# Hybrid decoder step: in the first sub-block, two spatial mixes and six folds of wo with the values are emitted later

## The chip, the core and the metric

The kernel runs on one core of one Trainium2 chip. Its time is the device time of one execution, in microseconds (us), as the median of several runs. The core has five engines that work side by side, each through its own instructions in a fixed order: PE multiplies matrices (PEld loads its stationary operand), DVE is the vector engine, ACT the scalar engine for activations and copies, POOL a second elementwise engine, and SP issues the DMAs.

## What is computed

One layer of a decoder in fp32, for 2048 new prompt tokens (D = 1024) and 32 sample tokens: a mixer with gated linear attention (GLA) and a spatial gating unit (SGU), a cross-attention to 256 memory tokens, and a gated MLP with a short convolution. The parts that the change touches:

```python
q, k, v, r, a, u, sv = split_cols(xn @ w_in)
...
o, S = gla_chunked(q, k, v, logg, s0)
o = rmsnorm(o, g_gla_out).astype(xn.dtype)
o = o.reshape(B, T, GLA_WIDTH) * jax.nn.silu(r)
u = jax.nn.gelu(u)
sv = rmsnorm(jax.nn.gelu(sv).reshape(B, T, SGU_HEADS, SGU_DH), g_sgu)
z = sgu_spatial(sv, w_s, b_s)
s_out = u * z.reshape(B, T, SGU_WIDTH)
y = jnp.concatenate([o, s_out], axis=-1) @ w_out
...
o = jnp.einsum('bhtm,bmhd->bthd', p, mv).reshape(B, T, D_MODEL)
return o @ wo_x
```

`sgu_spatial` multiplies, per head and per chunk of 128 tokens, a lower triangular 128x128 matrix with the normed values. The memory attention's last two lines are linear in the values, so the kernel multiplies the values by `wo_x` once, ahead of time, and uses the result as the weight for all tokens.

## The kernel before

The prompt is cut into four sub-blocks of 512 tokens (`s` = 0 to 3). Each sub-block goes through the projections, GLA and SGU, the output projection `wo`, the memory attention and the MLP. Products are made of three passes (`mm3`, lines 100 to 102): every fp32 operand is split into a high part and a residue (`split`, lines 85 and 86: ACT makes the high part, DVE or POOL the residue), and hi·hi, hi·lo and lo·hi are added up.

The program is written as a list of steps. `weave` takes a main list and side lists; a side list with (first, last) is spread evenly behind the main steps of these indices, and where several side lists are due behind the same main step, they follow in the order in which they are named. `run` goes through the woven list. It loads the weights of later steps up to five units ahead, and splits most of them as it loads them (`wunit`), so each weight brings a DMA on SP, an ACT instruction and a DVE instruction ahead of its step. The order in which the steps are emitted is not yet the order on an engine: the tile context is opened with `schedule_with_timeline_sim=True`, and when it is left, a pass orders each engine's instructions, with the emitted order as their priority. Each engine then runs its own in that order and waits on semaphores.

In the first sub-block the main list has 19 steps: the projections sv (0 to 3), a (4), k (5), q (6), v (7 to 10), u (11 and 12), r (13 to 16), and the first two half steps of `wo` (17 and 18), which take the SGU half of the concatenated input. Woven into it are:

- `qk_steps`: the folds of the queries' weight with the memory keys.
- `vo_steps`: eight folds of `wo_x` with the memory values, one for each head and each half of the columns (`fold_vo`). A fold reloads the head's values at its first half, and for two tiles of 128 rows makes six products of 512 columns (`vop`), evacuates them on ACT (`voh`) and DVE (`vol`), and leaves the writes to `vod` in DRAM, which SP issues later (`put` and `flush`). `vod` is read by the attention's output projection.
- `sgu_steps`: statistics and scaling of the values, then four spatial mixes, one per head (`mix`, from line 946 on). A mix makes four narrow products (`zp`, line 950), scales and shifts them on DVE (`z`, line 953), multiplies by u on POOL (line 958), and splits the result, the high part on ACT (`ch`) and the residue on POOL (`cl`). The SGU half of `wo` reads `ch` and `cl`.
- `gla_steps`: for each of two head pairs `p`, the diagonal, seven levels (0 to 6), a decay, the states and the chunk outputs. A level subtracts on DVE (`e`, line 1046), takes exponentials on ACT, makes `kr` (line 1058) and `e` times k (line 1062) on DVE, four products on PE for two heads together (`s`, line 1068; the profile counts eight instructions), and copies them under a mask to `P` on DVE (line 1072). The decay ends in POOL's `kh` (line 1104) and its transposes on PE (`ktp`, line 1107).
- `gtail`: norm (`onorm`), gating (`gate`) and transposes (`back`, `otp`, line 1217) of the GLA output, which the second half of `wo` needs.

Levels 2 to 6 and the decay of the second head pair are emitted behind main steps 12 and 13, its states and chunk outputs behind 16.

Of the kernel before, what the change touches and what calls it, by code (L numbers as in the profile page):

```python
# [38 lines left out]
def hymba_step_kernel(  # L39
# [22 lines left out]
    def U(name, dt=F32):  # L62
        return up.tile([128, TM], dt, tag="U", name=name)
# [63 lines left out]
    def wready(src, name):  # L127

        def load():
            out = []  # L130
            for x, tag in enumerate(("whi", "wlo")):
                t = wp.tile(list(src.shape[0:1]) + list(src.shape[2:]), F32R, tag=tag, name=f"{tag}_{name}")
                nc.sync.dma_start(t.bitcast(F32), src[:, x])
                out.append(t)
            return tuple(out)
        return load
# [220 lines left out]
    def keep(t, pattern, base, cm):  # L357
        pool.affine_select(out=t, in_=t, pattern=pattern, compare_op=ALU.is_ge, fill=0.0,
                           base=base, channel_multiplier=cm)
# [125 lines left out]
    def weave(main, *sides):  # L485

        out = []
        due = [0.0] * len(sides)
        at = [0] * len(sides)
        for i, m in enumerate(main):  # L490
            out.append(m)
            for j, (steps, first, last) in enumerate(sides):
                if i < first:
                    continue
                due[j] = len(steps) * min(1.0, (i - first + 1) / (last - first + 1))
                while at[j] < len(steps) and at[j] < due[j] - 1e-9:
                    out.append(steps[at[j]])
                    at[j] += 1
        for j, (steps, _, _) in enumerate(sides):
            out += steps[at[j]:]  # L500
        return out
# [158 lines left out]
    def fold_vo(h, jh, wu):  # L660

        if jh == 0:
            again("v", h)
        vh, vl = mem_st.t["v"]
        wh, wl = wu
        flush()
        for mt in range(2):
            ps = mps(f"vop{h}{jh}{mt}")
            for dt in range(2):
                a = dt * 256 + mt * 128  # L670
                mm3(ps, vh[:, a:a + 128], vl[:, a:a + 128], wh[:, dt], wl[:, dt], dt == 0, dt == 1)
            hi, lo = U(f"voh{h}{jh}{mt}", F32R), U(f"vol{h}{jh}{mt}", F32R)
            split(hi[:, :512], lo[:, :512], ps)
            kk = 2 * h + mt
            for x, t in enumerate((hi, lo)):
                put(vod[kk // 4][:, 2 * jh:2 * jh + 2, x, kk % 4],
                    t[:, :512].bitcast(F32).rearrange("p (m c) -> p m c", m=2))
# [7 lines left out]
    qk_steps = []  # L685
    for h, j in ((2 * i + hh, j) for i in range(2) for j in range(2) for hh in range(2)):
        qk_steps.append(Step(lambda a, h=h, j=j: turn_wq(h, j, a), [wraw_unit(wq_x[0], 4 * j, 4, h * 256, 256, f"wqf{h}{j}")]))
        qk_steps.append(Step(lambda h=h, j=j: fold_qk(h, j)))
    vo_steps = [Step(lambda a, h=h, jh=jh: fold_vo(h, jh, a), [(wo_x[0], 2 * h, 2, jh * 512, 512, f"wof{h}{jh}")])
                for h in range(4) for jh in range(2)]  # L690
# [155 lines left out]
    def carry_sample(B, prev):  # L846

        def fn():
            for k in range(8):
                pool.tensor_tensor(B.h[k][:, SB:TM], prev.h[k][:, SB:TM], smp.d[:, k * NS:(k + 1) * NS], ALU.add)  # L850
        return Step(fn)
# [903 lines left out]
    def final_steps(B):  # L1755
        s, sample = B.s, B.ffn_sample
        gfin = []

        def part(c):
            if c == 0:  # L1760
                for j in range(2):
                    t = U(f"gf{s}{j}")
                    nc.sync.dma_start(t[:, :512], g_final[j * 512:(j + 1) * 512].partition_broadcast(128))
                    gfin.append(t)
            n = 128 if c < 4 else NS
            dst = y_prompt[0, s * SB + c * 128:s * SB + (c + 1) * 128, :] if c < 4 else \
                y_sample.rearrange("b t d -> (b t) d")
            ss = narrow(f"yss{s}{c}")
            pss = []
            for j in range(2):  # L1770
                ps = mps(f"yp{s}{c}{j}")
                for i in range(4):
                    pe.transpose(ps[:n, i * 128:(i + 1) * 128], B.h[4 * j + i][:, c * 128:c * 128 + n], ident)
                act.activation(junk[:n], ps[:n], AF.Square, accum_out=ss[:n, j:j + 1])
                pss.append(ps)
            dve.tensor_tensor(ss[:n, 2:3], ss[:n, 0:1], ss[:n, 1:2], ALU.add)
            rstd_of(ss[:n, 3:4], ss[:n, 2:3], n, 1, 1.0 / D)
            for j in range(2):
                y = T_(f"y{s}{c}{j}")
                dve.scalar_tensor_tensor(y[:n, :512], pss[j][:n], ss[:n, 3:4], gfin[j][:n, :512], ALU.mult, ALU.mult)  # L1780
                nc.sync.dma_start(dst[:, j * 512:(j + 1) * 512], y[:n, :512])

        return [Step(lambda c=c: part(c)) for c in range(5 if sample else 4)]

    def conv_out_steps(src, n, dst, name):

        def part(j):
            nf = min(4, FT - 4 * j)
            ps = mps(f"{name}p{j}")
            for i in range(nf):  # L1790
                pe.transpose(ps[:n, i * 128:(i + 1) * 128], src[:, 4 * j + i, :], ident)
            t = T_(f"{name}t{j}")
            dve.tensor_copy(t[:n, :nf * 128], ps[:n, :nf * 128])
            nc.sync.dma_start(dst[:, j * 512:j * 512 + nf * 128], t[:n, :nf * 128])
        return [Step(lambda j=j: part(j)) for j in range(6)]
# [10 lines left out]
    steps = [Step(mem_norm)]  # L1806
    norm = norm_in_steps(blocks[0])
    steps += weave(mem_steps, (norm, 0, 11), ([Step(late_constants)], 2, 2))
    after = []
    for s, B in enumerate(blocks):  # L1810
        proj = proj_steps(B)
        gla, gtail = gla_steps(B)
        nlast = 4 if B.mix_sample else 3
        sgu_st = sgu_steps(B)
        nst = len(sgu_st) - 4
        keep = None
        if B.mix_sample:
            def keep():
                if not hasattr(smp, "x"):
                    smp.x = U("smpx")  # L1820
                return smp.x
        w1, w2, stat = out_proj_steps(B, lambda k0, m2, s=s: (w_out[0], k0, 4, m2 * 256, 256, f"wo{s}{k0}{m2}"),
                                      lambda B=B: B.cat, "gx", "wo", B.mix_sample, 4, B.mix_sample, keep, seven=True, whole=not B.mix_sample)
        early = [Step(sample_conv)] if B.ffn_sample else []
        folds = [(qk_steps, 0, 10), (vo_steps, 11, 19)] if s == 0 else []
        steps += weave(proj + w1, *folds, (after, 0, 5), (sgu_st[:1], 6, 6), (early, 1, 1), (sgu_st[1:nst], 11, 11), (sgu_st[nst:nst + 2], 12, 13), (sgu_st[nst + 2:], 16, 16), (gla[:1], 4, 4), (gla[1:2], 6, 6), (gla[2:12], 8, 10), (gla[12:-nlast], 10, 13), (gla[-nlast:], 16, 16), (gtail, 16, 18))
        scales, sc, turns = attention_steps(B)
        x1, x2, xstat = out_proj_steps(B, lambda k0, m2, s=s: wready(vod[k0 // 4][:, m2], f"wx{s}{k0}{m2}"),
                                       lambda B=B: B.ao, "gffn", "wx", False, 0, B.ffn_sample, seven=s > 0, whole=True)
        steps += w2 + [stat, scales]  # L1830
        steps += weave(sc + x1, (turns[:2], 8, 9), (turns[2:3], 13, 13), (turns[3:], 14, 14))
        fstart, fmain, flast = ffn_steps(B, s == NSB - 1)
        B.xstat = xstat.fn
        steps += x2 + ([xstat, fstart] if s == 0 else [])
        sides = []
        if B.mix_sample:
            sides.append((sample_steps(), 1, len(fmain) - 5))
        if s + 1 == NSB:
            ncs = conv_out_steps(carry, 2, o_state_conv[0, 0], "nc")
            sides.append((ncs[:4], 30, 36))  # L1840
        steps += weave(fmain[:-4], *sides)
        if s + 1 < NSB:
            after = final_steps(B)
            nxt = blocks[s + 1]
            norm = norm_in_steps(nxt)
            if nxt.ffn_sample:
                norm.append(carry_sample(nxt, B))
            steps += weave(fmain[-4:] + flast, (norm, 0, 4))
            if B.ffn_sample:
                after += conv_out_steps(sct, 16, o_state_conv_s[0].rearrange("b t f -> (b t) f"), "ncs")  # L1850
        else:
            steps += fmain[-4:-2] + flast[:1] + fmain[-2:] + ncs[4:] + flast[1:]
            after = []
# [30 lines left out]
```

## Time and profile before

| | |
|---|---|
| median of three runs | 2813.88 us (2811.18 to 2815.28) |
| the profiled execution | 2815.41 us |
| its span in the profile | 2813.7 us |
| mean granted clock | 0.995 |

The share of an engine's busy time is over the whole span. In a timeline, a row is a start, a length, an engine, a line and operation, output from inputs, a count, and in brackets how long the engine had stood idle and what ended that. Neighbouring instructions of one kind are merged into one row. A matmul's length overlaps with the next one's: the distance of starts is its cost. In a list of windows each engine has its busy time in that stretch and the number of its instructions, then follow the granted clock of PE, the share of the DMA engines and GB/s.

### The profile page before, as it was taken

Reading aid. Unit: us, or ns where it says so; the run is one execution under the profiler, and the core shown is the slowest. Engines: PE = TensorE matmul, PEld = TensorE weight load, DVE = VectorE, ACT = ScalarE, POOL = GpSimd, SP = SyncE. Lnnn points to the kernel's source line nnn. Section 1 sums busy time; section 2 is a strip of 40 time slices with the busy share of each in tenths; the row PEclk is TensorE's granted clock in tenths of the full one; section 3 lists DMA queues with packets and bytes.
Section 4 is the critical chain, followed back from the end, with each engine's and each line's share of the span. In section 5 each row is a group of like instructions: output and inputs, shape, how many; then the busy total and the mean of one; then the engine's idle time right before and its main releaser. Section 6 shows DMA issues by size and latency. Waiting matters only on the chain.

```text
span 2813.7 us, 46764 instructions
## 1 busy us (share of the span) xinstructions
PE 2773.2 (99%) x17746; PEld 2458.5 (87%) x17746; DVE 1897.5 (67%) x3296; ACT 1109.0 (39%) x1950; POOL 575.6 (20%) x640
## 2 busy tenths in 40 slices
PE   8999999999999999999999999999999999999998
PEld 8887888888878898898888889899999888899997
DVE  6677778777658885655545778666666688665555
ACT  5645545333354454222224445422223645421222
POOL 2002212111101221322211121232221013132222
PEclk9999999999999999999999999999999999999999
DMA  9765579999942245888995216577776324577775
GB/s 300 242 195 195 174 262 332 339 340 348 356 139 66 88 150 195 315 291 286 332 321 201 90 61 207 198 250 260 257 264 220 110 76 136 203 262 275 272 280 183
DMA packets 369546, 638.06 MB, mean 227 GB/s; under 512 B 27356, under 2 KB 238272, under 8 KB 369322
## 3 DMA queue, kind: packets, MB, share of 16 engines
q1 hardware_dynamic: 369322, 635.07, 66.2%
q8 instruction: 141, 2.31, 0.3%
q14 instruction: 83, 0.68, 0.1%
HBM read 507.56 MB, written 127.41 MB: 226 GB/s over the span
## 4 chain that ended last, share of the span: by engine, by line
PE 89%; DVE 5%; DMA 2%; ACT 2%; issue 1%; POOL 1%; SPq 0%; DVEq 0%; ACTq 0%; POOLq 0%
PE d L100 6%; PE d L102 6%; PE d L101 6%; PE a_wx L102 2%; PE a_wx L100 2%; PE a_wx L101 2%; PE s L1068 2%; PE a_wup L101 1%; PE a_wg L101 1%; PE a_wg L102 1%; PE a_wup L102 1%; PE a_wg L100 1%; PE a_wup L100 1%; PE a_wu L100 1%; PE a_wu L101 1%
## 5 line engine op out<-in xcount | busy, mean ns | idle before, releaser
L100 PE MATMUL d<-acth,whi_wd 128*128 128x272 f32 (+1 forms) x688 | 236.0, 343 | 1.1 <-DVE h L1732 1.1
L1732 DVE TENSOR_TENSOR h<-d,h 128x512 f32<-128x512 f32 (+1 forms) x232 | 133.5, 582 | 150.3 <-PE d L102 150.1
L101 PE MATMUL d<-actl,whi_wd 128*128 128x272 f32 (+1 forms) x688 | 233.4, 339 | 0.0
L102 PE MATMUL d<-acth,wlo_wd 128*128 128x272 f32 (+1 forms) x688 | 233.3, 340 | 0.0
L1625 POOL TENSOR_TENSOR c<-c,bc_f 128x512 f32<-128x512 f32 (+1 forms) x88 | 143.2, 1635 | 132.1 <-ACT c L1624 132.1
L1615 ACT ACTIVATE c<-g,colsb 128x512 f32<-128x512 f32 x88 | 71.7, 815 | 190.8 <-DVE g L1578 144.9
L100 PEld LDWEIGHTS d<-acth,whi_wd 128*128 128x128 f32 x688 | 129.4, 188 | 15.8 <-DVE h L1732 1.9
L102 PEld LDWEIGHTS d<-acth,wlo_wd 128*128 128x128 f32 x688 | 129.2, 188 | 15.6 <-issue 1.2
L101 PEld LDWEIGHTS d<-actl,whi_wd 128*128 128x128 f32 x688 | 129.5, 188 | 13.9 <-issue 0.4
L1647 POOL TENSOR_TENSOR c<-r_q_wup,c 128x512 f32<-128x512 f32 (+1 forms) x33 | 63.0, 1909 | 333.9 <-DVE r_q_wup L297 214.1
L1612 POOL COPY carry<-g 128x2 f32<-128x2 f32 x88 | 32.4, 369 | 417.9 <-DVE g L1578 413.8
L100 PE MATMUL a_wo<-ch,h_wo 128*128 128x512 f32 (+1 forms) x320 | 112.4, 364 | 2.8 <-ACT ch L89 1.8
L101 PE MATMUL a_wo<-cl,h_wo 128*128 128x512 f32 (+1 forms) x320 | 112.7, 355 | 0.0
L102 PE MATMUL a_wo<-ch,l_wo 128*128 128x512 f32 (+1 forms) x320 | 111.9, 352 | 0.0
L1616 DVE SCALAR_TENSOR_TENSOR c<-g,colsb,c 128x512 f32<-128x512 f32 x88 | 86.5, 983 | 28.4 <-ACT c L1615 27.8
L85 ACT ACTIVATE acth<-c 128x512 fp32r<-128x512 f32 (+1 forms) x88 | 55.7, 636 | 120.0 <-DVE c L1647 85.2
L102 PE MATMUL a_wx<-pTh,wlo_wx 128*128 128x512 f32 x256 | 101.2, 395 | 0.0
L101 PE MATMUL a_wx<-pTl,whi_wx 128*128 128x512 f32 x256 | 100.5, 393 | 0.0
L100 PE MATMUL a_wx<-pTh,whi_wx 128*128 128x512 f32 x256 | 100.2, 394 | 0.0
L1624 ACT ACTIVATE c<-c 128x512 f32<-128x512 f32 (+1 forms) x88 | 56.1, 637 | 83.7 <-DVE c L1617 71.7
L1617 DVE SCALAR_TENSOR_TENSOR c<-g,colsb,c 128x512 f32<-128x512 f32 x88 | 83.8, 952 | 1.1
L86 DVE TENSOR_TENSOR actl<-c,acth 128x512 fp32r<-128x512 f32 (+1 forms) x88 | 64.1, 733 | 25.6 <-ACT acth L85 24.5
(3753 smaller groups left out, 9693.3 us busy)
## 6 DMA issues: line engine op xcount, KB each, us to landing
whi_wd<-wd SPq DMA_DIRECT2D x66, 512.0 KB
wlo_wd<-wd SPq DMA_DIRECT2D x66, 512.0 KB
r_wo<-in_w_out_dram SPq DMA_DIRECT2D x32, 512.0 KB
wlo_wx<-vod SPq DMA_DIRECT2D x32, 512.0 KB
whi_wx<-vod SPq DMA_DIRECT2D x32, 512.0 KB
r_wg<-in_w_gate_dram SPq DMA_DIRECT2D x22, 512.0 KB
r_wup<-in_w_up_dram SPq DMA_DIRECT2D x22, 512.0 KB
r_wd<-in_w_down_dram SPq DMA_DIRECT2D x22, 512.0 KB
```

The source lines that it names most:

```text
L86: (lo_eng or dve).tensor_tensor(lo, src, hi.bitcast(F32), ALU.subtract)
L100: out = pe.matmul(ps, wh, xh, start=first, stop=False)
L101: pe.matmul(ps, wh, xl, start=False, stop=False)
L102: pe.matmul(ps, wl, xh, start=False, stop=last)
L1068: pe.matmul(ps3[:, :, c * 64:(c + 1) * 64], kl[:, c * 128:(c + 1) * 128], kr3[:, :, c * 64:(c + 1) * 64], start=True, stop=True)
L1615: act.activation(c[:, :SB], g[:, 2:SB + 2], AF.Identity, bias=cb, scale=w2)
L1616: dve.scalar_tensor_tensor(c[:, :SB], g[:, 1:SB + 1], w1, c[:, :SB], ALU.mult, ALU.add)
L1617: dve.scalar_tensor_tensor(c[:, :SB], g[:, 0:SB], w0, c[:, :SB], ALU.mult, ALU.add)
L1624: act.activation(c[:, :T], c[:, :T], AF.Gelu_apprx_tanh)
L1625: pool.tensor_tensor(c[:, :T], c[:, :T], B.fbc[:, :T], ALU.mult)
L1647: (dve, pool)[i].tensor_tensor(c[:, :T], q[i], c[:, :T], ALU.mult)
L1732: dve.tensor_tensor(B.h[m + mm][:, cs], ps[:, :cw], B.h[m + mm][:, cs], ALU.add)
```

## The change

In the first sub-block (`s == 0`) two side lists get other places. The folds 0 and 1 stay behind main steps 11 and 12; folds 2 to 7, one behind each of steps 13 to 18 until now, go behind steps 15 (two), 16 (one), 17 (two) and 18 (one). The spatial mixes 0 and 1, behind steps 12 and 13 until now, both go behind step 15, where they follow folds 2 and 3. Mixes 2 and 3 stay behind step 16. In the other sub-blocks nothing is changed. No instruction is added or removed.

```diff
-        folds = [(qk_steps, 0, 10), (vo_steps, 11, 19)] if s == 0 else []
-        steps += weave(proj + w1, *folds, (after, 0, 5), (sgu_st[:1], 6, 6), (early, 1, 1), (sgu_st[1:nst], 11, 11), (sgu_st[nst:nst + 2], 12, 13), (sgu_st[nst + 2:], 16, 16), (gla[:1], 4, 4), (gla[1:2], 6, 6), (gla[2:12], 8, 10), (gla[12:-nlast], 10, 13), (gla[-nlast:], 16, 16), (gtail, 16, 18))
+        folds = [(qk_steps, 0, 10), (vo_steps[:2], 11, 12), (vo_steps[2:], 15, 18)] if s == 0 else []
+        steps += weave(proj + w1, *folds, (after, 0, 5), (sgu_st[:1], 6, 6), (early, 1, 1), (sgu_st[1:nst], 11, 11), (sgu_st[nst:nst + 2], *((12, 13) if s else (15, 15))), (sgu_st[nst + 2:], 16, 16), (gla[:1], 4, 4), (gla[1:2], 6, 6), (gla[2:12], 8, 10), (gla[12:-nlast], 10, 13), (gla[-nlast:], 16, 16), (gtail, 16, 18))
```

## The prediction

> **What bounds the kernel now.** I read the page's busy shares first, then PE's waits in the part of the span that the change touches, then that part by windows, then the timelines of PE, DVE and POOL at the longest wait.
>
> ```profile
> span 2813.7 us, 46764 instructions
> PE 2773.2 (99%) x17746; PEld 2458.5 (87%) x17746; DVE 1897.5 (67%) x3296; ACT 1109.0 (39%) x1950; POOL 575.6 (20%) x640
> ```
>
> PE is busy 2773.2 of 2813.7 us, so a change that neither adds nor removes a product can gain only where PE stands still or runs slowly. The profiled execution took 2815.41 us, 1.7 us more than its span and 1.5 us above the median of the runs, 2813.88 us. What the sum takes off the profiled execution I take off the median too. 0.2% is 5.6 us, which is also about what a measurement of this kernel can tell from no change (the three runs spread over 4.1 us).
>
> PE's waits from 180 to 330 us (total, times, longest), and the same stretch by windows:
>
> ```profile
> PE s L1068 <- DVE kr L1058: 5.0, 2, 3.3
> PE otp L1217 <- DVE vol L86: 2.4, 1, 2.4
> PE ktp L1107 <- POOL kh L1104: 0.9, 1, 0.9
> PE otp L1217 <- DVE o L1211: 0.7, 1, 0.7
> ```
>
> ```profile
> 214.00:247.00 33.00, 33.00 (x168) 27.74 (x168) 25.20 (x40) 17.14 (x32) 4.84 (x3) 1.00 0.60 192
> 247.00:258.00 11.00, 5.08 (x21) 4.18 (x20) 10.84 (x17) 3.45 (x6) 3.40 (x3) 0.63 0.30 95
> 258.00:264.00 6.00, 6.00 (x18) 4.75 (x17) 1.43 (x3) 0.94 (x2) 0.00 (x0) 0.54 0.25 84
> 264.00:270.00 6.00, 6.00 (x33) 5.12 (x32) 4.42 (x5) 5.24 (x8) 0.00 (x0) 1.00 0.79 258
> 270.00:281.00 11.00, 11.00 (x67) 9.06 (x67) 7.56 (x14) 5.89 (x10) 6.23 (x5) 1.00 0.97 340
> 281.00:293.00 12.00, 11.89 (x68) 9.94 (x66) 11.17 (x20) 7.00 (x11) 2.89 (x2) 1.00 0.68 202
> 293.00:302.00 9.00, 5.53 (x19) 4.22 (x20) 5.71 (x9) 2.74 (x5) 1.01 (x1) 0.81 0.75 257
> ```
>
> The columns after the stretch's length are PE, PEld, DVE, ACT, POOL, the granted clock and DMA. There are two holes: PE works 5.08 of 11 us up to 258, and 5.53 of 9 us up to 302. In the first, DVE is busy 10.84 of 11 us: PE waits for a DVE that is late, not for data. The first hole's waits are the longest of PE in this stretch. Its rows on PE:
>
> ```profile
> 239.61 1.06 PE L1068 MATMUL s<-kr,e 128*128 128x128 f32 x8
> ...
> 246.97 0.40 PE L102 MATMUL t_wr<-h_wr,xl 128*128 128x512 f32 x1
> 250.64 2.05 PE L1068 MATMUL s<-kr,e 128*128 128x128 f32 x8 [3.28 <-DVE kr L1058]
> 254.42 2.05 PE L1068 MATMUL s<-kr,e 128*128 128x128 f32 x8 [1.73 <-DVE kr L1058]
> 257.39 1.12 PE L1107 MATMUL ktp<-ident,kh 128*128 128x128 f32 x4 [0.92 <-POOL kh L1104]
> 258.16 0.78 PE L100 MATMUL vop<-h_wof,vr 128*128 128x512 f32 x1
> ...
> 263.42 0.43 PE L100 MATMUL vop<-h_wof,vr 128*128 128x512 f32 x1
> ...
> 266.21 0.39 PE L100 MATMUL vop<-h_wof,vr 128*128 128x512 f32 x1
> ```
>
> After the last product of r, PE has levels 5 and 6 of the second head pair next in its order. Folds that could fill the gap stand behind them: 36 products (three folds) follow from 258.16 on. The same eight products of a level that took 1.06 us at 239.61 take 2.05 us in the hole, and the twelve products of one fold take 5.26 us (258.16 to 263.42) where the next twelve take 2.79 us (263.42 to 266.21): the granted clock, 1.00 before, is 0.63 and 0.54 in these windows.
>
> Why DVE is late, on DVE and on POOL:
>
> ```profile
> 235.68 0.43 DVE L1062 TENSOR_TENSOR e<-e,k 128x256 f32<-128x256 f32 x1 [0.48 <-ACT e L1048]
> 237.52 1.23 DVE L86 TENSOR_TENSOR l_wof<-r_wof,h_wof 128x1024 fp32r<-128x1024 f32 x1
> ...
> 242.72 0.69 DVE L86 TENSOR_TENSOR vol<-vop,voh 128x512 fp32r<-128x512 f32 x1 [1.24 <-ACT voh L85]
> ...
> 244.72 0.75 DVE L953 SCALAR_TENSOR_TENSOR z<-zp,colsb,bsb 128x512 f32<-128x512 f32 x1
> 245.37 0.68 DVE L1046 TENSOR_TENSOR e<-b 128x512 f32<-128x512 f32 x1
> 245.97 2.32 DVE L86 TENSOR_TENSOR l_wo<-r_wo,h_wo 128x1024 fp32r<-128x1024 f32 x1
> 248.22 1.48 DVE L1062 TENSOR_TENSOR e<-e,k 128x256 f32<-128x256 f32 x1
> ```
>
> ```profile
> 224.99 2.14 POOL L958 TENSOR_TENSOR z<-z,u 128x512 f32<-128x512 f32 x1 [35.45 <-DVE z L953]
> ...
> 245.60 1.61 POOL L958 TENSOR_TENSOR z<-z,u 128x512 f32<-128x512 f32 x1 [16.42 <-DVE z L953]
> 247.96 1.46 POOL L86 TENSOR_TENSOR cl<-z,ch 128x512 fp32r<-128x512 f32 x1 [0.74 <-ACT ch L85]
> ...
> 274.21 2.66 POOL L86 TENSOR_TENSOR cl<-z,ch 128x512 fp32r<-128x512 f32 x2 [0.79 <-ACT ch L85]
> ```
>
> Level 5 opens at 245.37, behind a fold's two residues (0.69 each, the first from 242.72 after 1.24 us in which DVE waits for it) and mix 1's z (0.75). Then mix 1's two POOL operations lie exactly over two DVE operations: l_wo takes 2.32 instead of 1.23 us beside POOL's z, and level 5's product with k 1.48 instead of 0.43 us beside POOL's cl. So the fold and the mix at this place cost level 5 about 242.72 to 245.37, that is 2.7 us, and 1.1 + 1.05 = 2.1 us of stretching: 4.8 us, about the 5.0 us that PE waits.
>
> [...]
>
> **Removed, added, moved.** Nothing is computed more or less. In the first sub-block the spatial mixes 0 and 1 go from indices 12 and 13 of the woven list to 15, and folds 2 to 7 from 13–18 to 15–18 (two, one, two, one). So levels 2 to 6 and the decay of the second head pair, emitted at 12 and 13, have only fold 1 beside them and no mix. The emitted order is a priority; the compiler's timeline pass fixes each engine's order from it.
>
> *The levels.* Fold 2's residues and mix 1's z leave the place ahead of level 5, mix 0's z and its POOL work (2.14 us from 224.99) the place ahead of level 2: levels 5 and 6 come at least the 4.8 us earlier worked out above. What is late next? DVE's work up to the last product of r was 25.20 of 33 us. Less two residues and two z (2 × 0.69 + 2 × 0.75 = 2.9), plus what fell behind it (10.84, less the 2.1 us of stretching, about 8.7), it is 31.0 us. PE's window shrinks by one fold (2.79) and two mixes (eight products like a level's, 16 narrow products, about 2 × 1.06) and grows by two levels (2 × 1.06): 33 − 2.8 = 30.2 us. DVE therefore just about keeps up; the rest is 0.8 us and lies under the folds, which PE now finds behind the r products. *Value taken: both waits for kr and the one for kh go, 3.28 + 1.73 + 0.92 = 5.93 us. Bounds: 0 (PE's order still puts levels 5 and 6 first and they are as late) and 5.93.*
>
> *The clock.* Without the gap the products that follow run at full clock: 2 × (2.05 − 1.06) = 1.98 us for the two levels and 5.26 − 2.79 = 2.47 us for the fold, together 4.45 us. The bounds are 0 and 4.45, as for the wait that causes it. [...] In the trace PE is busy from 258.16 and slow until 263.42, 5.3 us, so the row decides.
>
> *The folds.* Each brings one 512 KB load, one split of it (DVE 1.23 as in l_wof), two reloads of the values when a head begins, 12 products, two evacuations on ACT and two residues on DVE, and four writes on SP. All go along: on SP the r weights pass the loads of folds 2 and 3, so that r cannot starve; the fold weights come later, but three folds already ran behind the hole. The results are needed only by the attention's output projection, far behind. I cost this at nothing, the cover being three folds of PE work; if that cover were gone, a late weight would cost PE one split, 1.2 us. From below: no gain, as the work is the same.
>
> *The mixes.* All four now stand behind the levels. Their chain is DVE, POOL, ACT, POOL. The rows show two of them, one behind the other:
>
> ```profile
> 268.94 1.95 PE L950 MATMUL zp<-wsT,sv 128*128 128x128 f32 x16
> ```
>
> From 268.94 to 274.21 + 2.66 = 276.87 is 7.9 us for two, so about 16 us for four. The first wo product needs the first two, the last quarter of the pass all four. If their products come first behind the levels, three folds (3 × 2.79 = 8.4 us) cover the first pair: cost 0. If they come behind folds 2 and 3, one fold and the other pair's products (2.79 + 1.95) cover 4.7 of 7.9 us: PE waits 3.2 us. [...] I take the middle, 1.6 us, since no row says which order the pass chooses.
>
> **Sum:** 5.93 + 4.45 − 1.6 = 8.8 us gained. 2815.41 − 8.8 = 2806.6 us for the profiled execution; 2813.88 − 8.8 = 2805.1 us for the median.
>
> **Rivals.** *Given back at the second hole (no change).* Behind 281 us DVE is busy 11.17 of 12 us with the gated linear attention's tail (norm, gate, transposes), and PE then waits 2.4 + 0.7 us for it. If that tail ends when it does now, PE only arrives earlier and waits longer: 2813.9 us, within 2 us. For it speaks the full DVE; against it, that DVE idles 35 − 1.43 − 4.42 − 7.56 − 11.17 = 10.4 us from 258 to 293, mostly under the slow folds, and that the tail's start hangs on PE's order. Chance 0.18.
>
> *The order does not follow (no change).* If the pass leaves levels 5 and 6 straight behind the last r product and the folds behind them, only the 4.8 us ahead of level 5 can go, 2813.9 − 4.8 = 2809.1 us; if DVE's other splits take the vacated places, nothing goes, 2813.9 us. For it: the pass placed them so already. Against it: what fills the gap is now emitted ahead of the fourth step of r. Chance 0.09.
>
> *Slower: the moved DVE work lands in the tail.* One fold more now follows the states of the second pair, and four mixes run close together. If two residues, two z and the POOL stretching (2 × 0.69 + 2 × 0.75 + 3 × 1.1 = 6.2 us; the third stretch is that of 224.99) fall behind 281 us, where DVE has 0.83 us to spare, the last gate comes 5.4 us later; and if the levels gain nothing, PE waits that long at the transposes. The products behind such a gap run at about half clock, at least another fold's 2.5 us: 2813.9 + 5.4 + 2.5 = 2821.8 us. It decides once more than the 0.8 us lands there while the first hole stays. Against it: 10.4 us of DVE idle time lie ahead of 293, and mixes and folds 2 and 3 are emitted ahead of the tail. Chance 0.16. [...]
>
> **How the numbers follow.** The forecast has 0.57. The faster end: both holes go. The second is 3.1 us of waits and a clock of 0.81 over 9 us, 0.19 × 9 = 1.7 us; 8.8 + 1.6 + 4.8 = 15.2 us, 2798.7 us, rounded down to 2798. At the other end the range takes in no change and the spread, and the milder part of the slower case: 2817 us. It leaves out about 0.12 above and 0.05 below. Given forecast alone I would say 2799 to 2809. Faster by over 0.2% (below 2808.3 us) 0.57, within 0.27 (0.18 + 0.09), slower 0.16.
>
> **What would show it.** Right: no wait of s for kr over 1 us around 250, the granted clock 1.00 from 214 to 280, folds or mixes on PE between the last r product and the transposes of kh, level 5's e ahead of 242, mixes 0 and 1 on POOL at the end of the levels, and the second hole 7 to 10 us earlier, no longer than 4 us. Wrong: the hole still ahead of levels 5 and 6; a new wait of the wo products for ch or cl of mixes over 3.2 us; or the wait at otp grown by what the first hole lost. A difference outside 180 to 330 us would mean that the pass reordered other stages, which I have costed at nothing.

## The result, and the profile after

The changed kernel takes 2799.72 us (median of five runs, 2798.88 to 2799.95), the kernel before 2813.54 us in the same comparison (2811.18 to 2815.28). The ratio is 0.9951 with a 95% interval of 0.9941 to 0.9962: 13.8 us faster, where 8.8 us were forecast. The profiled execution has a span of 2798.0 us.

PE's waits from 180 to 330 us, in the changed kernel (total, times, longest):

```profile
PE a_wo L100 <- ACT r L898: 2.0, 1, 2.0
PE s L1068 <- DVE o L1157: 0.7, 1, 0.7
PE otp L1217 <- DVE vol L86: 0.6, 1, 0.6
PE a_wo L100 <- ACT ch L89: 0.6, 1, 0.6
```

The waits for kr and kh are gone, those at the transposes (otp) have shrunk from 3.1 to 0.6 us, and a new one has come, wo for the Silu of r. With 0.5 us before, and 0.6 now, in which wo waits for a ch of the GLA output, 9.5 us in all became 3.9. The same stretch by windows, with the columns as before:

```profile
214.00:247.00 33.00, 33.00 (x169) 27.78 (x169) 28.01 (x50) 19.32 (x29) 1.62 (x1) 1.00 0.59 184
247.00:258.00 11.00, 10.22 (x73) 8.84 (x71) 6.20 (x7) 5.54 (x7) 7.44 (x5) 1.00 0.88 284
258.00:264.00 6.00, 4.80 (x14) 3.83 (x15) 3.64 (x8) 4.89 (x9) 4.55 (x4) 0.72 0.59 194
...
270.00:281.00 11.00, 11.00 (x57) 9.30 (x57) 10.33 (x18) 6.55 (x10) 2.57 (x3) 1.00 0.64 194
281.00:293.00 12.00, 10.78 (x54) 8.47 (x53) 8.62 (x13) 5.87 (x9) 1.91 (x1) 1.00 1.00 350
293.00:302.00 9.00, 9.00 (x41) 7.30 (x40) 7.63 (x11) 6.01 (x10) 3.79 (x3) 1.00 0.54 171
```

Of the seven windows one has a clock below 1.00. DVE now does 28.01 us of work up to 247 us (25.20 before). On PE, the levels of the second head pair stand among the r products, and folds and mixes follow them:

```profile
233.37 1.05 PE L1068 MATMUL s<-kr,e 128*128 128x128 f32 x8
236.35 1.05 PE L1068 MATMUL s<-kr,e 128*128 128x128 f32 x8
239.10 0.60 PE L1107 MATMUL ktp<-ident,kh 128*128 128x128 f32 x4
...
247.15 1.05 PE L950 MATMUL zp<-wsT,sv 128*128 128x128 f32 x8
...
259.20 0.73 PE L100 MATMUL a_wo<-ch,h_wo 128*128 128x512 f32 x1 [1.98 <-ACT r L898]
```

Levels 5 and 6 are at 233.37 and 236.35 instead of 250.64 and 254.42 us. That is 17 and 18 us earlier, far more than the 4.8 us of the prediction's step. The first product of the memory attention's scores, a name that occurs once in the program, tells what the stage as a whole gained. The rows of the tile sc00A (minimum, median and maximum length in ns, first and last start), of the kernel before and of the changed one:

```profile
L100 PE MATMUL sc00A<-whi_qk00A,w1wo x8: 278/284/287, 332.3 to 336.1; 128*128 128x256 f32 x8
```

```profile
L100 PE MATMUL sc00A<-whi_qk00A,w1wo x8: 278/280/287, 320.2 to 324.0; 128*128 128x256 f32 x8
```

It comes 12.1 us earlier. Of this, 1.3 us were there already ahead of the change: the last products of the query folds came at 184.4 instead of 185.7 us, and the granted clock from 20 to 35 us was 1.00 instead of 0.89. So the stage itself gained 10.8 us: 5.6 us of waits and some 5 us of clock. The span shrank by 15.7 us. About 2 us of that came in the second sub-block, whose code was not touched. PE's waits there (940 to 1060 us before, 926 to 1046 now) are 4.2 us in both kernels, though at other places: the kernel before waits 1.6 us in one piece at the transposes of the sample mixer, and then has a clock of 0.83 from 990 to 1000 us, about 1.7 us lost; in the changed kernel this wait is gone and the clock stays at 1.00. That the pass went on from another state and so changed the order there is likely and not shown. For the rest (1.5 us between 340 and 940 us) I have no cause; it appears against this execution of the kernel before in e1 and e2 alike, and this execution is 1.9 us above the median of its runs.

### The profile page after: what moved, and what is told of

Its sections match the earlier page's. It is cut to its first block, busy times and chain, and to the rows that moved or that the text cites. A ratio compares the mean times of both kernels' runs of the same rounds, so it can differ in the third digit from the quotient of the medians.

```text
span 2798.0 us, 46773 instructions
## 1 busy us (share of the span) xinstructions
PE 2765.6 (99%) x17746; PEld 2453.0 (88%) x17746; DVE 1897.2 (68%) x3296; ACT 1110.5 (40%) x1952; POOL 574.0 (21%) x640
## 4 chain that ended last, share of the span: by engine, by line
PE 92%; DVE 4%; DMA 2%; ACT 1%; issue 1%; POOL 1%; DVEq 0%; SPq 0%; ACTq 0%; POOLq 0%
PE d L101 6%; PE d L100 6%; PE d L102 6%; PE a_wx L102 2%; PE a_wx L101 2%; PE a_wx L100 2%; PE s L1068 2%; PE a_wo L100 2%; PE a_wo L101 2%; PE a_wo L102 2%; PE a_wg L101 1%; PE a_wup L101 1%; PE a_wg L102 1%; PE a_wup L102 1%; PE a_wg L100 1%; PE a_wup L100 1%
```

## Experiments

All times are medians beside runs of the kernel before on the same chip, 2813.1 to 2813.3 us. The diffs are against the changed kernel for e1 to e4, e8 and e10, and against the kernel before for the others; they show only the part of a line that changes. Where a run is compared with the changed kernel, the latter's time is the 2799.72 us above; the last group has it beside the others, as e9.

**Which of the two moves did it: e1 and e2.**

```diff
-(sgu_st[nst:nst + 2], *((12, 13) if s else (15, 15)))
+(sgu_st[nst:nst + 2], 12, 13)
```

> Folds 2 to 7 moved as in the changed kernel, mixes 0 and 1 left behind steps 12 and 13. Theory A (fold 2 and mix 1 share the delay of level 5, as predicted): the fold's 2 us of the 4.8 us go and the folds fill the gap, 4 to 6 us faster than before. Theory B (the mixes alone hold the levels back, through the order that the pass makes; the folds only matter for the second hole): the wait of s for kr stays at 5 us or grows, since the r products run out earlier without fold 2 among them; at most the second hole's 3 to 5 us go.

```diff
-(vo_steps[:2], 11, 12), (vo_steps[2:], 15, 18)
+(vo_steps, 11, 19)
```

> Mixes 0 and 1 moved as in the changed kernel, the folds left behind steps 11 to 18. Theory A: mix 1's z and the stretching go, 2.9 of the 4.8 us, with half of the clock's loss 4 to 6 us faster than before, the levels still behind the r products. Theory B: the levels come 12 us earlier as in the changed kernel, no wait of s for kr, 8 to 10 us faster, and the second hole (2.4 + 0.7 us of waits before the transposes, clock 0.8) stays.

The folds alone gave 2807.69 us, ratio 0.9982 (0.9973 to 0.9992), the mixes alone 2802.80 us, 0.9962 (0.9947 to 0.9977): 5.4 and 10.3 us. e1's three longest waits on PE:

```profile
PE otp L1217 <- DVE vol L86: 2.3, 2, 1.2
PE ktp L1107 <- POOL kh L1104: 2.3, 1, 2.3
PE s L1068 <- ACT h_wof L85: 2.1, 1, 2.1
```

With the folds alone, the levels stay at the end of the r products, and the hole shrinks from 5.9 to 4.4 us without closing. This is theory A's number, though not its picture, and theory B's wait for kr of 5 us or more did not come. e2's waits:

```profile
PE otp L1217 <- DVE vol L86: 2.6, 2, 2.5
PE s L1068 <- DVE o L1157: 0.7, 1, 0.7
...
PE otp L1217 <- DVE o L1211: 0.3, 1, 0.3
```

With the mixes alone the first hole is gone altogether and the second is as before, as theory B had it. The 10.3 us are close to what the prediction gave for the first hole, 5.93 + 4.45 = 10.4 us. The folds add 3.5 us to that (13.8 − 10.3), at the second hole. So the mixes alone would have done for the first.

**How the mixes hold the levels back: e5, e6, e7, e12.** On DVE, the subtraction that opens levels 1 and 2 and the z of mix 0, in the kernel before:

```profile
202.33 0.68 DVE L1046 TENSOR_TENSOR e<-b 128x512 f32<-128x512 f32 x1
...
224.10 0.75 DVE L953 SCALAR_TENSOR_TENSOR z<-zp,colsb,bsb 128x512 f32<-128x512 f32 x1 [1.13 <-PE zp L950]
...
225.90 1.79 DVE L1046 TENSOR_TENSOR e<-b 128x512 f32<-128x512 f32 x1
```

and in the changed kernel:

```profile
200.95 0.68 DVE L1046 TENSOR_TENSOR e<-b 128x512 f32<-128x512 f32 x1
...
203.27 0.68 DVE L1046 TENSOR_TENSOR e<-b 128x512 f32<-128x512 f32 x1
...
225.22 0.68 DVE L1046 TENSOR_TENSOR e<-b 128x512 f32<-128x512 f32 x1
```

All that these subtractions read is there at the first of them. Yet before, level 2 opens 23.6 us after level 1, behind mix 0's z and one split; level 5 opens just behind mix 1's z (244.72 and 245.37, in the prediction). In the changed kernel level 2 follows level 1 after 2.3 us, and level 5 opens at 225.22. Two DVE operations of 0.75 us cannot do that. z and e are tiles of the same pool, T, with six buffers. Theory C: the pass hands these out in emitted order, so a level that is emitted behind a mix gets no tile until the mix's z has its own, and z is written only when its products are done. e5 leaves everything in its place and gives z another pool:

```diff
-            z = T_(f"z{s}{h}")
+            z = (U if s == 0 and h < 2 else T_)(f"z{s}{h}")
```

> The kernel before, with mixes and folds where they were, and only the z of mixes 0 and 1 in a tile of the large pool U instead of the pool T, from which the levels take e and kr. Theory C (the tiles of a pool are handed out in emitted order, so level 2 cannot get its tile before mix 0's z and level 5 not before mix 1's z, and z waits for its products and a bank): the levels come 10 us or more earlier although nothing moved, no wait of s for kr, 8 to 11 us faster than before. Theory A (the mixes' own DVE and POOL work at this place delays level 5): the work stays where it was, so the wait of 5 us stays within 2 us and the time within 4 us of before.

It takes 2801.04 us, ratio 0.9956 (0.9941 to 0.9971), 12.3 us faster than before with neither mix nor fold moved, more than theory C's 8 to 11. Its rows on DVE:

```profile
203.39 0.68 DVE L1046 TENSOR_TENSOR e<-b 128x512 f32<-128x512 f32 x1
...
226.42 0.74 DVE L953 SCALAR_TENSOR_TENSOR z<-zp,colsb,bsb 128x512 f32<-128x512 f32 x1
...
227.74 1.40 DVE L1046 TENSOR_TENSOR e<-b 128x512 f32<-128x512 f32 x1
```

Level 2 opens at 203.39, 23 us ahead of mix 0's z. Level 5's subtraction even runs beside mix 0's POOL work (1.40 instead of 0.68 us), and PE doesn't wait for kr at all. Theory A is out: the mixes' work is still there, beside the levels. The transposes wait only 0.3 us, so the second hole has closed too, without a fold having moved.

e6 removes the stretching that the prediction made part of the hole:

```diff
-            pool.tensor_tensor(z[:, :SB], z[:, :SB], B.u[h][:, :SB], ALU.mult)
+            off = s == 0 and h < 2
+            (dve if off else pool).tensor_tensor(z[:, :SB], z[:, :SB], B.u[h][:, :SB], ALU.mult)
...
-            split(hi[:, :T], lo[:, :T], z[:, :T], pool)
+            split(hi[:, :T], lo[:, :T], z[:, :T], dve if off else pool)
```

> The kernel before, with the product with u and the residue of mixes 0 and 1 of the first sub-block on DVE instead of POOL, so that no POOL operation lies over level 5's DVE operations; DVE gets four more operations of about 0.7 us. If the stretching (2.1 us) is a real part of the first hole, level 5's product with k takes 0.43 us instead of 1.48, the waits for kr shrink by 1 to 2 us net of the added DVE work and the time falls by 1 to 4 us. If it was only in the shadow of the place in the order (theory C), the waits stay at 5 us and the time within 2 us of before.

2813.94 us, ratio 1.000 (0.9991 to 1.001). Its DVE around level 5 (the lines are one higher here):

```profile
245.16 0.74 DVE L953 SCALAR_TENSOR_TENSOR z<-zp,colsb,bsb 128x512 f32<-128x512 f32 x1
245.81 0.68 DVE L1047 TENSOR_TENSOR e<-b 128x512 f32<-128x512 f32 x1
246.41 1.22 DVE L86 TENSOR_TENSOR l_wo<-r_wo,h_wo 128x1024 fp32r<-128x1024 f32 x1
247.55 0.68 DVE L959 TENSOR_TENSOR z<-z,u 128x512 f32<-128x512 f32 x1
248.15 0.41 DVE L1063 TENSOR_TENSOR e<-e,k 128x256 f32<-128x256 f32 x1
```

The stretching was real and is gone: l_wo 1.22 instead of 2.32 us, level 5's product with k 0.41 instead of 1.48. But the level opens behind z as before, PE waits 5.2 us for kr as before (5.0), and the mixes' four operations fill the time on DVE. So moving this work to DVE gains nothing. What the stretching alone costs e6 can't tell, since it puts the same work on DVE; but in e5 DVE operations are stretched as well (the 1.40 us above), and PE doesn't wait for kr.

e7 moves mix 1 alone:

```diff
-(sgu_st[nst:nst + 2], 12, 13)
+*([(sgu_st[nst:nst + 2], 12, 13)] if s else [(sgu_st[nst:nst + 1], 12, 12), (sgu_st[nst + 1:nst + 2], 15, 15)])
```

> The kernel before, with mix 1 alone behind step 15. Theory C: levels 2 to 4 stay late, behind mix 0's z; levels 5 and 6 no longer wait for mix 1's z, the first hole closes to under 1 us of waits, 7 to 10 us faster than before. Theory A with both mixes sharing the delay: about half of it, 4 to 6 us.

2800.22 us, ratio 0.9950 (0.9933 to 0.9966): 13.1 us, more than theory C's 7 to 10. Level 2's products are at 236.84 us (235.05 before), late as forecast, and levels 5 and 6 follow at 246.94 and 248.53 with no wait. The transposes wait 0.4 us, so the second hole has closed too. I had not expected that from moving one mix. As in e5 the folds are emitted where they were, and no run tells which shift in the order did it.

e12 asks whether six tiles are simply too few:

```diff
-NU, NT, NRAW, NW = 49, 6, 5, 5
+NU, NT, NRAW, NW = 48, 7, 5, 5
```

> The kernel before with seven tiles in pool T instead of six, and 48 instead of 49 in pool U to make room. If the levels are held back because six tiles are too few, they come earlier and the first hole closes, 8 us or more. Theory C (the order in which the tiles are handed out, not their number): levels 5 and 6 stay behind the r products, PE waits for kr 3 us or more, and the time is within 4 us of before.

2807.23 us, ratio 0.9982 (0.9973 to 0.9991), so 6.0 us faster; both numbers that I had given for theory C, a wait of 3 us and a time within 4 us, were missed. Its rows:

```profile
221.83 0.75 DVE L953 SCALAR_TENSOR_TENSOR z<-zp,colsb,bsb 128x512 f32<-128x512 f32 x1 [1.15 <-PE zp L950]
223.63 1.78 DVE L1046 TENSOR_TENSOR e<-b 128x512 f32<-128x512 f32 x1
...
240.69 0.74 DVE L953 SCALAR_TENSOR_TENSOR z<-zp,colsb,bsb 128x512 f32<-128x512 f32 x1
241.34 0.68 DVE L1046 TENSOR_TENSOR e<-b 128x512 f32<-128x512 f32 x1
```

Levels 2 and 5 still open behind the two z as before. In this execution level 1 had already opened 2.3 us earlier than in the kernel before (200.04 instead of 202.33 us), so level 2 again follows it after 23.6 us, with seven tiles as with six. So a seventh tile doesn't undo the order, which is the point of theory C. Level 5 comes 4.0 us earlier, 1.7 us more than level 1, and PE's first hole shrinks to 0.3 us for level 6 and 1.8 us for kh. What the seventh tile did there was not tried.

**The second hole and the new wait: e3, e4, e8.**

```diff
-(vo_steps[2:], 15, 18)
+(vo_steps[2:], 15, 17)
```

> The changed kernel with folds 2 to 7 spread over steps 15 to 17 instead of 15 to 18, so that fewer products stand between the states and the transposes. If folds behind the states are what closes the second hole (PE has work while DVE finishes the tail), PE waits 2 to 3 us at the transposes again and the time is 2 to 5 us above the changed kernel. If the hole closed because the tail as a whole begins earlier, the time stays within 1 us.

2803.99 us, ratio 0.9967 (0.9954 to 0.9980), 4.3 us above the changed kernel's 2799.72. PE waits 2.2 and 1.7 us at the transposes:

```profile
PE otp L1217 <- DVE o L1211: 2.2, 1, 2.2
PE a_wo L100 <- ACT r L898: 2.1, 1, 2.1
PE otp L1217 <- DVE vol L86: 1.7, 1, 1.7
```

In the changed kernel the last folds therefore close the second hole: they are PE's work while DVE finishes the tail. They are not the only thing that can, as e5 and e7 showed.

The new wait for r has its chain in the changed kernel (start, length, what; the short pieces between them, in which nothing on record is waited for, are left out):

```profile
253.33 2.21 POOL z L958
...
255.57 0.04 ACT ch L85
...
256.11 1.04 ACT h_wof L85
...
257.16 1.28 ACT L898
...
258.46 0.70 ACT r L898
...
259.20 0.73 PE a_wo L100
```

On ACT, mix 1's ch stands ahead of the Silu of r and of a table load at the Silu's line (1.28 us), and waits 2.67 us for POOL. The products of r and of wo take their tiles from one pool of four, acc, and by the profile the first wo product was released by the Silu of r, after 1.98 us. So the wait comes through ACT's order and not as a lack of ch. In e2 both mixes stand behind the same step, with the folds at their old places, and PE doesn't wait for r at all; so the place of the mixes alone does not make this wait. e4 puts the mixes one step further forward, still behind the levels:

```diff
-(15, 15)
+(14, 14)
```

> The changed kernel with mixes 0 and 1 behind step 14, ahead of folds 2 and 3 but still behind the levels. If the new wait of wo for r (2.0 us, with a half clock of about 1.6 us behind it) comes from ACT standing at mix 1's ch until POOL is done, with the Silu of r queued behind, the mixes are now done earlier, the wait shrinks below 1 us and the time falls 2 to 4 us below the changed kernel. If the wait comes from the activation table and the banks alone, it stays and the time is within 1 us.

2798.00 us, ratio 0.9944 (0.9930 to 0.9959). The wait for r is gone from the list, but 2.2 us of waits have come back at the transposes, so only 1.7 us are left of the 2 to 4 expected; the interval overlaps with the changed kernel's. e8 adds later folds:

```diff
-(vo_steps[2:], 15, 18)
+(vo_steps[2:4], 15, 15), (vo_steps[4:], 17, 18)
...
-(15, 15)
+(14, 14)
```

> Mixes 0 and 1 behind step 14 and folds 4 to 7 behind steps 17 and 18, so that 24 fold products in a row stand ahead of the tail's transposes. If the second hole is a lack of PE work ahead of the transposes, its 2.2 us of waits and its lower clock go, and the time is 2 to 4 us below the run with mixes behind 14 (2798.0 us). If the tail is bound by DVE, the residues of these folds push it back and the wait at the transposes stays at 2 us or grows.

2797.49 us, ratio 0.9943 (0.9928 to 0.9958). All of PE's waits of this stretch:

```profile
PE s L1068 <- DVE o L1157: 0.7, 1, 0.7
PE a_wo L100 <- ACT ch L89: 0.7, 1, 0.7
PE sc00S L102 <- DVE wtlwo L86: 0.4, 1, 0.4
PE sc00A L102 <- DVE w1wo L86: 0.3, 1, 0.3
```

Both holes are closed, but the time is only 0.5 us below e4's, inside the spread of the runs, where 2 to 4 us were expected.

**Side by side on one chip: e9, e10, e11.** e9 is the changed kernel, e10 the kernel of e8. e11 needs no move of the mixes:

```diff
-folds = [(qk_steps, 0, 10), (vo_steps, 11, 19)] if s == 0 else []
+folds = [(qk_steps, 0, 10), (vo_steps[:4], 11, 14), (vo_steps[4:], 17, 18)] if s == 0 else []
...
-            z = T_(f"z{s}{h}")
+            z = (U if s == 0 else T_)(f"z{s}{h}")
```

> The changed kernel, unchanged, beside the next one on the same chip. All theories: 2799 to 2801 us.

> Mixes 0 and 1 behind step 14 and folds 4 to 7 behind steps 17 and 18, again. If its second hole is closed and the wait of wo for r is gone for good, 1.5 to 3.5 us below the changed kernel of the same call; if the earlier difference was the spread of the runs, within 1 us.

> The z of all four mixes of the first sub-block in a tile of pool U, mixes at their old places, folds 0 to 3 behind steps 11 to 14, folds 4 to 7 behind 17 and 18. Theory C: the levels need no move of the mixes, so both holes are closed and the time is within 2 us of the kernel with mixes behind 14 and late folds. Theory A: the mixes beside the levels cost the first hole again, 2806 us or more.

| | median, us | runs, us | ratio to before (95%) |
|---|---|---|---|
| e9 | 2800.26 | 2796.78 to 2800.61 | 0.9952 (0.9939 to 0.9964) |
| e10 | 2796.16 | 2795.52 to 2798.79 | 0.9944 (0.9930 to 0.9958) |
| e11 | 2798.62 | 2795.88 to 2801.74 | 0.9949 (0.9937 to 0.9962) |

The kernel of e8 and e10 has the lowest median both times (2.2 and 4.1 us below the changed kernel, the latter more than expected), but runs and intervals overlap, so that it beats the changed kernel is likely and not shown. e11 is 2.5 us from e10, a little outside the expected 2, and far below theory A's 2806: with another pool for z, mixes that stay beside the levels cost nothing that these runs can tell.

## Why the prediction was right, and where it was not

- *The first hole bounds this stage.* Right. Its size, 5.93 us of waits and 4.45 us of clock, is about what e2 gained with this hole closed and the second left (10.3 us).
- *"Levels 5 and 6 come at least the 4.8 us earlier".* Right in sign, wrong in mechanism. Level 5 opened at 225.22 instead of 245.37 us. The 4.8 us were made of the operations just ahead of level 5 and of the stretching behind its start, and they matched the wait of 5.0 us by chance: e6 removes the stretching and gains nothing, e5 leaves the mixes' operations and removes the hole. The step that failed is the reading of DVE's rows as a queue of work. The 23.6 us between levels 1 and 2 with nothing to wait for were in the trace before, and I did not look for them. What holds them is the shared pool of tiles (e5); the order rather than the number of tiles is argued from e5 and e12 and not shown alone.
- *The folds at nothing.* Too careful: in the changed kernel they closed the second hole (3.5 us beyond e2; e3 brings it back). The forecast left that hole as it was and had its closing only in the range's lower end. This is the largest missing term.
- *The mixes at 1.6 us.* A cost came, but of another kind and larger: 1.98 us of waiting for r, and in the profiled execution eight wo products at 0.43 instead of 0.23 us, about 1.6 us more, 3.6 us together. In e9, the same kernel, the wait is there and the slow products are not. My estimate had no clock in it, and no run shows a wait of 3.2 us of wo for the mixes, nor what the clock does behind one. The margin that I computed, folds covering the mixes' chain, was not what decided; ACT's order was, and not by the mixes' place alone (with it e2 has no such wait).
- *Nothing outside the stage.* Wrong by about 2 us in the second sub-block, most of it clock, in this case to the good.
- *The rivals.* The tail did not keep its end: its last gate came at 284.57 instead of 295.81 us, and the otp waits shrank to 0.6 us. The order followed. The slower case did not come either, but not because DVE had time to spare: while the tail ran, DVE was busy 10.33 of 11 us (270 to 281). The tail began and ended earlier with the levels, and PE had the last folds to do meanwhile.
- *The signs.* Level 5's e came ahead of 242 us and no wait for kr was left. The clock of 1.00 up to 280 us was missed (0.72 from 258 to 264), and so was the place of the kh transposes: at 239.10 us they stand among the r products and not behind them.

The sum by terms in the stage: 10.4 us at the first hole as forecast (before the mixes' cost), about 4 at the second instead of 0 (2.5 us of waits and 1.7 us of clock), less 3.6 instead of 1.6: 10.8 us, where 8.8 were forecast. Two misses of opposite sign kept the sum near. The other 3.0 of the 13.8 us lie outside the stage, where the forecast had nothing.

## What to carry to other kernels

When an instruction whose inputs are all there starts late and close behind another one, look for a shared pool of tiles before adding up the work around it: giving the z of two mixes another pool (e5) did nearly all that moving eight steps did, 12.3 of 13.8 us. A step that can run at any time, such as the last folds, can close a hole where an engine with nothing to do waits for another one's chain: with the last folds spread up to step 17 instead of 18 (e3), PE waits 2.2 and 1.7 us at the transposes, in the changed kernel 0.6 us. But e5 and e7 closed the same hole with the folds emitted as before: what fills a hole is read from the order in the trace, not from the emitted one. Look also at what stands behind an operation that waits, in its engine's order: here mix 1's ch waited 2.67 us for POOL, the Silu of r stood behind it on ACT, and PE stood 1.98 us for the Silu.

## What the hardware showed besides

The clock behind the same wait was lower in one execution and not in another. In the profiled execution of the changed kernel PE stood 1.98 us before the first wo product, the products behind it started 0.43 us apart, and the window of 258 to 264 us has a clock of 0.72. e9 is the same kernel once more, with the same wait:

```profile
258.89 0.50 PE L100 MATMUL a_wo<-ch,h_wo 128*128 128x512 f32 x1 [1.98 <-ACT r L898]
```

```profile
258.00:264.00 6.00, 5.11 (x23) 4.24 (x24) 3.34 (x8) 4.58 (x9) 4.57 (x4) 1.00 0.63 214
```

Here the clock stayed at 1.00 and the products behind the wait started 0.23 us apart. So the 1.6 us of clock belong to that execution and not to the kernel. In e3 PE stood 2.1 us at the same place and the clock stayed at 1.00 too:

```profile
258.00:264.00 6.00, 4.25 (x19) 3.51 (x20) 2.98 (x3) 5.99 (x10) 0.12 (x1) 1.00 0.72 245
```

So a single gap of 1.98 us was followed by the lower clock in one of two executions of the same kernel, and e3's gap of 2.1 us was not. What decides it is not shown.
